# A decoder layer in three float32r passes: where its split weights and activations lie modulo 512 bytes

## The chip, the core and the metric

The kernel runs on one core of one Trainium2 chip. The metric is the device time of one execution in microseconds. Before the change it is 1091.87 us, the median of 3 runs (1091.37 to 1092.54). The profile is of one further execution.

## The reference, cut to what matters

One decoder layer on 256 tokens of width 2048: an input projection, eight heads of dilated window attention and eight heads of latent attention, an output projection, and an MLP with a squared ReLU, each between two RMSNorms. All inputs are float32.

```python
h = _rmsnorm(x, norm_attn_pre)
a_q, a_k, a_v, c_q, c_kv, k_r = split(h @ w_in)        # 2048 -> 3*1024 + 512 + 512 + 64
a_out = dilated window attention of (a_q, a_k, a_v)    # 8 heads x 128
q_b = _rmsnorm(c_q) @ w_uq; kv = _rmsnorm(c_kv) @ w_ukv
b_out = causal attention of (q_b, kv, k_r)             # 8 heads x 128
x = x + _rmsnorm(concat(a_out, b_out) @ w_out, norm_attn_post)   # 2048 -> 2048
h = _rmsnorm(x, norm_mlp_pre)
u = square(relu(h @ w_up))                             # 2048 -> 8192
x = x + _rmsnorm(u @ w_down, norm_mlp_post)            # 8192 -> 2048
```

## The kernel before

**Three passes.** A float32 product is carried by three float32r passes. Each operand is split exactly into a part of 12 significant bits, called hi, and the rest, called lo; hi*hi, lo*hi and hi*lo are added up in PSUM. ScalarE (ACT) writes hi by a copy that rounds (L234), VectorE (DVE) writes lo as source minus hi (L235). For three tiles of the first chunk of `w_up` GpSimd (POOL) writes lo instead (`POOL_U`).

**Which operand is which.** The activations are the stationary operand: 128 tokens by 128 of the inner dimension, loaded into TensorE (PE) by a weight load, which the profile calls LDWEIGHTS and lists under the engine PEld. There is one such load for every matmul. The weights of the model are the moving operand: 512 columns of a split tile stream past (288 for the latent projection, 384 for `w_uq`). So while a matmul streams 2048 bytes of a split weight tile from each partition, the weight load of the next matmul reads 512 bytes of an activation from the same partition.

**Weight tiles.** There are 377 weight tiles, numbered in the order of use, of 1024 columns by 128 partitions in float32 (4096 bytes a partition) or less. `Weights.emit` loads tile i into one of 5 raw buffers with a DMA on SP's queue, then issues its split into one of 8 hi and 8 lo buffers (`W_BUFS`). `Weights.get(i)` is called when tile i is used, and emits up to tile i + 6 (`W_AHEAD`; 4 around the norms of the residual, `AHEAD_NORM`), but never more than `limit` = 8 tiles past the first one that isn't finished.

**Order.** The order on each engine is written out by hand. `proj` emits the matmuls of a chunk tile by tile, first for the token block 0 and then for block 1, and `Flow` puts the short steps of attention heads and norms between them. In the last chunk of `w_out` the last 5 tiles, and in the first of `w_up` the first 7, are used by block 0 as a whole before block 1 uses them (`APART`), so that `residual(0)` and `residual(1)` can run on DVE, ACT and POOL beside the matmuls. The MLP's down projection keeps its whole output in 8 PSUM banks (`y`); in its last group of 8 tiles (`g` = 15, tiles 369 to 376) each bank is finished by itself, and ACT squares it and DVE scales it while PE works on the next.

**Where tiles lie.** Tiles of a pool lie one behind the other in each partition: pools on the left side grow from low addresses, pools on the right from the top. In the program that is built from this kernel the addresses are, modulo 512 bytes:

| tile | role | residue |
|---|---|---|
| hi and lo of every weight tile | moving | 352 |
| `xT` hi and lo (q, k, v, latents) | stationary | 384 |
| `cqT` hi and lo (`w_uq`) | stationary | 384 |
| `mixT` hi and lo (`w_ukv`, `w_out`) | stationary | 480 |
| `hT` hi and lo (`w_up`) | stationary | 352 |
| `u` hi and lo (`w_down`) | stationary | 352 |

Steps inside a tile are multiples of 512 bytes, except in the latent projection, whose second half starts 1152 bytes on. So the distance from the moving to the stationary operand, modulo 512, is 32 for q, k, v, c_q and `w_uq`; 32 and 416 in turn for the latent c_kv; 128 for `w_ukv` and `w_out`; and 0 for the whole MLP.

Of the kernel before, what the change touches and what calls it, by code (L numbers as in the profile page):

```python
"""One decoder layer: dilated sliding-window heads and latent-attention heads side by side,
then a squared-ReLU MLP, each between two RMSNorms.

Float32 products are carried by three float32r passes: an operand is split exactly into
hi (12 significant bits) and lo (the rest), and hi*hi + hi*lo + lo*hi are accumulated.
Activations are the stationary operand (128 tokens), weights move 512 columns at a time.

The three dilated configurations share their scores, so their merged output is one softmax
in which a key counts once for each configuration that sees it: exp(s) * n = exp(s + ln n).
"""  # L10
# [44 lines left out]
def shape_constants():  # L55
    """Rotary frequencies and attention biases: they depend on the shapes alone."""
    fa = (THETA ** (-np.arange(0, RA, 2, dtype=np.float64) / RA)).astype(np.float32)
    fb = (THETA ** (-np.arange(0, RB, 2, dtype=np.float64) / RB)).astype(np.float32)
    freq = np.concatenate([-fa, fa, -fb, fb, fa, fa, fb, fb])
    i = np.arange(P)[:, None] + P  # L60
    j = np.arange(2 * P)[None, :]
    dist = i - j
    count = np.zeros((P, 2 * P))
    for window, dil in CONFIGS:
        count += (dist >= 0) & (dist <= window) & (dist % dil == 0)
    bias_a = np.where(count > 0, np.log(np.maximum(count, 1)) / SCALE_A, NEG)
    bias_b = np.where(dist >= 0, 0.0, NEG)
    out = np.concatenate([np.broadcast_to(freq, (P, 192)), bias_a, bias_b], axis=1)
    return np.ascontiguousarray(out.astype(np.float32))


# Weight tiles: raw ones that loads fill ahead, split ones, and how far ahead of their use they are
# split. AHEAD_NORM: the same while the norms around the residual need the vector engine; POOL_U:
# tiles of that stretch whose lo part gpsimd computes.
RAW_BUFS, W_BUFS, W_AHEAD, AHEAD_NORM = 5, 8, 6, 4
POOL_U = (3, 5, 7)
# Tiles in which block 0 goes before block 1: the last of w_out, the first of w_up.
APART = (5, 7)
# The first tiles are split by k-tile, and their lo parts are used last.
FINE = 6  # L80
FIRST_KPTS = [1, 1] + [2] * 7
# x^T by pieces: k-tiles, and the weight tiles loaded by then.
X_PIECES = ((1, 1), (1, 2), (2, 3), (3, 4), (3, 6), (3, 7), (3, 7))
# Products of zeros that raise the tensor engine's clock while the first loads are on their way.
# [3 lines left out]
# Pauses between the steps of a chain, by the flow's clock. DA, DB: a head's, after the transposes,  # L88
# the scores, the maximum, the exponentials, the normalisation, the probabilities' transpose.
# [11 lines left out]
class Flow:  # L101
    """Order of emission: projections fill the tensor engine, and chains of short dependent
    steps (an attention head, a norm) put their steps between them, each a while after the last."""
# [26 lines left out]
    def until(self, reached):  # L130
        """Emit steps of chains until this holds."""
        while not reached():
            c = min(self.chains, key=lambda c: c[0])
            self.clock = max(self.clock, c[0])
            self._step(c)

    def finish(self, *chains):
        """Emit until these chains have ended."""
        self.until(lambda: not any(c in self.chains for c in chains))


class Weights:
    """Weight tiles in the order of their use: loaded and split some tiles ahead."""
# [11 lines left out]
    def emit(self, upto):  # L155
        upto = min(upto, self.done.index(False) + self.limit, len(self.specs))
        while len(self.tiles) < upto:
            i = len(self.tiles)
            src, nk, n = self.specs[i]
            raw = self.pool.tile([P, CW], F32, tag="raw", bufs=RAW_BUFS, name=f"raw{i}")  # L160
            hi = self.pool.tile([P, CW], F32R, tag="hi", bufs=self.bufs, name=f"hi{i}")
            lo = self.pool.tile([P, CW], F32R, tag="lo", bufs=self.bufs, name=f"lo{i}")
            w = nk * n

            def v(t):
                return t[:, :w].rearrange("p (k n) -> p k n", k=nk)

            self.nc.sync.dma_start(out=v(raw), in_=src.rearrange("(k p) n -> p k n", p=P))
            cuts = [(k * n, (k + 1) * n) for k in range(nk)] if i < FINE else [(0, w)]
            for o, e in cuts:  # L170
                self.split_fn(hi[:, o:e], lo[:, o:e], raw[:, o:e], i in self.on_pool)
            self.tiles.append((v(hi), v(lo)))
# [9 lines left out]
class Chunk:  # L182
    """512 or so columns of a weight: its tiles as (index, first k-tile, k-tiles)."""
# [9 lines left out]
    def plan(self, n):  # L193
        """Put the next n tiles into the order of use."""
        for kp in self.kpts[len(self.tiles):len(self.tiles) + n]:
            k = sum(self.kpts[:len(self.tiles)])
            src = self.src[k * P:(k + kp) * P, self.c0:self.c0 + self.n]
            self.tiles.append((self.weights.plan(src, kp, self.n), k, kp))


def layer(nc, tc, io):
# [5 lines left out]
    con = pool("con", "left")  # L207
    xp = pool("xp", "left")
# [64 lines left out]
    def in_order(n, apart=(0, 0)):  # L273
        """(tile, block) pairs; block 0 goes before block 1 in the first and the last `apart` tiles."""
        f, l = apart[0], n - apart[1]
        return ([(t, b) for b in range(NB) for t in range(f)] + [(t, b) for t in range(f, l) for b in range(NB)]
                + [(t, b) for b in range(NB) for t in range(l, n)])

    def proj(aT, chs, name, order=None, need=None):
        """tokens x chunks into PSUM; yields (chunk, block, banks) as each ends."""  # L280
# [31 lines left out]
    def rstd_of(ss, n, width, name):  # L312
        """(sum / width + eps) ** -0.5, [128, n]."""
# [10 lines left out]
    xT = [pa.tile([P, KD, S], F32R, name=f"xT_{w}") for w in ("hi", "lo")]  # L324
    gcol = con.tile([P, 8], F32, name="gcol")
# [13 lines left out]
    def x_piece(k0, nk):  # L339
        """k-tiles of x^T, each with its gain as the last column."""  # L340
# [40 lines left out]
    def tables():  # L381
        """Rotary tables: sin (its first half negated) and cos, [128, block, 96] each."""
# [22 lines left out]
    def rope(tmp_pool, dst, src, half, nh, first, name):  # L405
        """dst, src [128, block, nh, 2 * half]; tables from column `first`."""
# [12 lines left out]
    def softmax_pv(wk, dl, sc, bias, scale, v, head, name):  # L419
        """sc [128, 384]: scores of block 0 on keys 0..127, then of block 1 on keys 0..255."""  # L420
# [83 lines left out]
    def latent(c, i, n, pl):  # L504
        """Transposed latent with its gain, split; its norm's factor goes on after the product."""
# [27 lines left out]
    # shared rotary key, in the upper or the lower 64 rows, zero elsewhere  # L533
# [14 lines left out]
    latT["q"] = [pb.tile([P, 4, S], F32R, name=f"cqT_{w}") for w in ("hi", "lo")]  # L548
    q_chain = flow.start(latent(cq, 1, "q", pb), 2.0)
# [84 lines left out]
    def residual(b):  # L634
        """x += y * rstd * gain; x * gain of the next norm, transposed and split."""
# [42 lines left out]
    for ns in ((0, 1), (2,), (3,)):  # L678
# [4 lines left out]
        for c, b, acc in proj(mixT, [ch_o[n] for n in ns], f"o{ns[0]}", order, heads_done):  # L683
            n = ns[c]
            if not late:
# [4 lines left out]
                late["hT"] = [hp.tile([P, KD, S], F32R, name=f"hT_{w}") for w in ("hi", "lo")]  # L690
# [22 lines left out]
    def split_u(g):  # L713
        if g == 0:
            uh, ul = [wp.tile([P, CW], F32R, tag=w, bufs=W_BUFS, name=f"u{w}0").rearrange("p (k s) -> p k s", k=4)
                      for w in ("hi", "lo")]
        else:
            uh, ul = [dpl["dp"].tile([P, 4, S], F32R, tag=f"u{w}", bufs=2, name=f"u{w}{g}") for w in ("hi", "lo")]
        split(uh.rearrange("p k s -> p (k s)"), ul.rearrange("p k s -> p (k s)"), uT[g].rearrange("p k s -> p (k s)"))
        return uh, ul  # L720
# [27 lines left out]
    def down_mm(u, g, kk, b, ns):  # L748
        """One k-tile into these 512 columns, ns in one tile of the weight."""
# [9 lines left out]
    def spare(i, n):  # L759
        """512 columns in two uT tiles that have been used."""  # L760
# [9 lines left out]
    def final(b):  # L770
        """The last columns' square closes the sum; x += y * gain * rstd."""
# [66 lines left out]
def arrays_of(inputs):  # L838
    """The inputs as the kernel reads them: x also transposed, with its gain; other gains by column."""
# [29 lines left out]
```

## Time and profile before

| what | value |
|---|---|
| median of 3 runs | 1091.87 us |
| the profiled execution, first to last instruction (span) | 1089.3 us |
| PE busy | 1074.7 us, 4978 matmuls |
| PEld busy | 890.1 us, 4978 weight loads |
| DVE busy | 568.0 us |
| ACT busy | 526.9 us |
| POOL busy | 14.2 us |
| DMA | 203.09 MB, mean 186 GB/s |
| mean granted TensorE clock | 0.996 |

Times are in microseconds from the start of the span. A matmul's duration in a row contains its way through the array, which overlaps the next matmul; what a stream of matmuls costs is the distance between their starts, called the pitch below. Busy PE is the union of such durations and says nothing of the pitch. A row with "x2" or "x4" merges that many instructions. "PEclk" is the clock that TensorE was granted, as a share of full speed.

### The profile page before, as it was taken

What the parts mean: (1) busy time and instruction counts of PE and PEld (TensorE: products, weight loads), DVE (VectorE), ACT (ScalarE), POOL (GpSimd) and SP (SyncE); (2) the same over time, 40 slices, a digit from 0 to 9 for tenths busy, and PEclk for the clock granted to TensorE, in tenths of its full rate; (3) what the DMA queues carried; (4) which work ended last, traced back from release to release, by engine and by line L of the source; (5) the groups of instructions that cost most, each with busy time, mean ns of one, the idle gap of its engine ahead of it and who ended that gap; (6) DMA issues with size and microseconds to landing.
All of it is one profiled execution on the core that took longest, in us unless ns stands there. A gap on an engine that the chain in (4) does not pass through costs nothing.

```text
span 1089.3 us, 13045 instructions
## 1 busy us (share of the span) xinstructions
PE 1074.7 (99%) x4978; PEld 890.1 (82%) x4978; DVE 568.0 (52%) x706; ACT 526.9 (48%) x700; POOL 14.2 (1%) x20
## 2 busy tenths in 40 slices
PE   9999999999999899999999999999999999999996
PEld 6888889888888688888888888888888888888885
DVE  6576446477554864444444444445544454445444
ACT  6655446565453464554445544454444444444442
POOL 0000000000000300000000000000000000000000
PEclk9999999999999999999999999999999999999998
DMA  9874546455376376566665666646655567655532
GB/s 318 304 251 146 145 125 214 149 167 166 100 257 205 97 232 181 168 191 196 191 181 169 189 198 191 185 165 208 195 193 193 192 193 232 194 194 194 193 119 78
DMA packets 89967, 203.09 MB, mean 186 GB/s; under 512 B 6832, under 2 KB 11440, under 8 KB 89648
## 3 DMA queue, kind: packets, MB, share of 16 engines
q1 hardware_dynamic: 89472, 201.89, 58.7%
q8 instruction: 39, 0.64, 0.3%
q10 hardware_dynamic: 432, 0.37, 0.1%
q14 instruction: 24, 0.20, 0.0%
HBM read 200.13 MB, written 2.10 MB: 186 GB/s over the span
## 4 chain that ended last, share of the span: by engine, by line
PE 97%; issue 1%; DVE 1%; DMA 1%; ACT 0%; POOL 0%; DVEq 0%; POOLq 0%; ACTq 0%
PE y L226 31%; PE acc_u L226 31%; PE acc_o L226 8%; PE acc_v L226 4%; PE acc_k L226 4%; PE acc_q L226 4%; PE acc_ckv L226 2%; PE acc_cq L226 2%; PE acc_ukv L226 2%; PE acc_uq L226 2%; PE rt L230 1%; PE sc_b L226 1%; PE sc_a L226 0%; PE o_a L226 0%; PE o_b L226 0%
## 5 line engine op out<-in xcount | busy, mean ns | idle before, releaser
L235 DVE TENSOR_TENSOR lo<-raw,hi 128x1024 fp32r<-128x1024 f32 (+3 forms) x378 | 447.4, 1190 | 445.9 <-ACT hi L234 444.8
L234 ACT ACTIVATE hi<-raw 128x1024 fp32r<-128x1024 f32 (+3 forms) x381 | 387.9, 1026 | 344.3 <-PE y L226 180.1
L226 PE MATMUL acc_u<-hi,hT_hi 128*128 128x512 f32 x512 | 203.3, 397 | 0.0
L226 PE MATMUL acc_u<-hi,hT_lo 128*128 128x512 f32 x512 | 200.1, 391 | 0.0
L226 PE MATMUL acc_u<-lo,hT_hi 128*128 128x512 f32 x512 | 199.8, 390 | 0.0
L226 PE MATMUL y<-hi,uhi 128*128 128x512 f32 x512 | 199.4, 389 | 0.0
L226 PE MATMUL y<-lo,uhi 128*128 128x512 f32 x512 | 199.2, 389 | 0.0
L226 PE MATMUL y<-hi,ulo 128*128 128x512 f32 x512 | 160.3, 389 | 0.0
L226 PEld LDWEIGHTS acc_u<-hi,hT_lo 128*128 128x128 f32 x512 | 96.4, 188 | 20.6
L226 PEld LDWEIGHTS y<-hi,ulo 128*128 128x128 f32 x512 | 96.1, 188 | 20.1
L226 PEld LDWEIGHTS y<-hi,uhi 128*128 128x128 f32 x512 | 96.1, 188 | 19.9
L226 PEld LDWEIGHTS y<-lo,uhi 128*128 128x128 f32 x512 | 96.1, 188 | 19.9
L226 PEld LDWEIGHTS acc_u<-lo,hT_hi 128*128 128x128 f32 x512 | 96.6, 189 | 19.0
L226 PEld LDWEIGHTS acc_u<-hi,hT_hi 128*128 128x128 f32 x512 | 96.5, 188 | 18.9
L226 PE MATMUL acc_o<-hi,mixT_hi 128*128 128x512 f32 x128 | 52.3, 409 | 0.0
L226 PE MATMUL acc_o<-hi,mixT_lo 128*128 128x512 f32 x128 | 50.6, 396 | 0.0
L226 PE MATMUL acc_o<-lo,mixT_hi 128*128 128x512 f32 x128 | 50.5, 394 | 0.0
L736 ACT ACTIVATE r<-acc_u,rstd_pre 128x512 f32<-128x512 f32 x32 | 21.9, 689 | 53.5 <-PE acc_u L226 53.5
L226 PEld LDWEIGHTS acc_o<-hi,mixT_lo 128*128 128x128 f32 x128 | 24.1, 188 | 6.0 <-DVE mixT_lo L235 0.4
L226 PEld LDWEIGHTS acc_o<-hi,mixT_hi 128*128 128x128 f32 x128 | 24.1, 189 | 5.1 <-ACT mixT_hi L234 0.2
L226 PEld LDWEIGHTS acc_o<-lo,mixT_hi 128*128 128x128 f32 x128 | 24.2, 189 | 4.9
L711 ACT ACTIVATE uT<-rt 128x512 f32<-128x512 f32 x32 | 19.1, 597 | 17.2 <-PE rt L230 17.1
(192 smaller groups left out, 1019.2 us busy)
## 6 DMA issues: line engine op xcount, KB each, us to landing
raw<-in_w_up SPq DMA_DIRECT2D x128, 512.0 KB, 4.2
raw<-in_w_down SPq DMA_DIRECT2D x128, 512.0 KB, 4.5
raw<-in_w_in SPq DMA_DIRECT2D x55, 512.0 KB, 5.0
raw<-in_w_out SPq DMA_DIRECT2D x32, 512.0 KB, 4.3
raw<-in_w_in SPq DMA_DIRECT2D x16, 288.0 KB, 2.8
raw<-in_w_ukv SPq DMA_DIRECT2D x8, 512.0 KB, 4.3
raw<-in_w_uq SPq DMA_DIRECT2D x8, 384.0 KB, 3.3
x<-in_x SPq DMA_DIRECT2D x8, 256.0 KB, 6.2
```

The costliest lines, as they stand in the source:

```text
L226: nc.tensor.matmul(out, a, b, start=start, stop=stop)
L230: nc.tensor.transpose(out, a, ident)
L234: nc.scalar.activation(hi, src, AF.Copy)
L235: (nc.gpsimd if pool else nc.vector).tensor_tensor(out=lo, in0=src, in1=hi.bitcast(F32), op=OP.subtract)
L711: nc.scalar.activation(uT[j][:, :, b * P:(b + 1) * P], t.rearrange("p (k s) -> p k s", k=4), AF.Square)
L736: nc.scalar.activation(r, acc[0], AF.Relu, scale=rstd2[b])
```

## The change

Three things are changed; the rest of the diff takes out comments and docstrings (some as blank lines), so that line numbers move by up to 9.

```diff
-RAW_BUFS, W_BUFS, W_AHEAD, AHEAD_NORM = 5, 8, 6, 4
+RAW_BUFS, W_BUFS, W_AHEAD, AHEAD_NORM = 5, 7, 6, 4
+SHIFT, H_LO, U_HI, U_LO = 16, 8, 4, 12
...
-            hi = self.pool.tile([P, CW], F32R, tag="hi", bufs=self.bufs, name=f"hi{i}")
-            lo = self.pool.tile([P, CW], F32R, tag="lo", bufs=self.bufs, name=f"lo{i}")
+            s = i % 8 * SHIFT
+            hi = self.pool.tile([P, CW + 8 * SHIFT], F32R, tag="hi", bufs=self.bufs, name=f"hi{i}")[:, s:s + CW]
+            lo = self.pool.tile([P, CW + 8 * SHIFT], F32R, tag="lo", bufs=self.bufs, name=f"lo{i}")[:, s:s + CW]
...
     con = pool("con", "left")
+    con.tile([P, 32], F32, name="con_pad")
...
+    pa.tile([P, 104], F32, name="pa_pad")
...
+    pb.tile([P, 104], F32, name="pb_pad")
...
-                late["hT"] = [hp.tile([P, KD, S], F32R, name=f"hT_{w}") for w in ("hi", "lo")]
+                late["hT"] = [hp.tile([P, KD * S + s], F32R, name=f"hT_{w}")[:, s:].rearrange("p (k s) -> p k s", k=KD)
+                              for w, s in (("hi", 0), ("lo", H_LO))]
...
         if g == 0:
-            uh, ul = [wp.tile([P, CW], F32R, tag=w, bufs=W_BUFS, name=f"u{w}0").rearrange("p (k s) -> p k s", k=4)
-                      for w in ("hi", "lo")]
+            uh, ul = [wp.tile([P, CW + 8 * SHIFT], F32R, tag=w, bufs=W_BUFS, name=f"u{w}0")[:, s:s + CW]
+                      for w, s in (("hi", U_HI), ("lo", U_LO))]
         else:
-            uh, ul = [dpl["dp"].tile([P, 4, S], F32R, tag=f"u{w}", bufs=2, name=f"u{w}{g}") for w in ("hi", "lo")]
+            uh, ul = [dpl["dp"].tile([P, CW + 128], F32R, tag=f"u{w}", bufs=2, name=f"u{w}{g}")[:, s:s + CW]
+                      for w, s in (("hi", U_HI), ("lo", U_LO))]
```

**The residues.** A buffer for a split tile is 512 bytes longer, and tile i starts (i mod 8) times 64 bytes into it. With the pads the weights lie at 480, 32, 96, 160, 224, 288, 352 and 416 in turn, `xT`, `cqT`, `mixT` and the hi part of `hT` at 480, the lo part of `hT` at 0, `u` hi at 496 and `u` lo at 16. The distance from moving to stationary operand then takes, about equally often, the 8 multiples of 64 in the projections up to `w_out`; the multiples of 64 (two matmuls in three) and 32 more (one in three) in `w_up`; and 16 and 48 more than a multiple of 64 in `w_down`.

**The buffers.** 7 hi and 7 lo buffers in place of 8, and with them `limit` = 7.

**The order.** PE and SP execute the same instructions in the same order as before. On the other engines the smaller `limit` moves these: the split of tile 123 (the third of `w_up`) goes behind ACT's first square of the last `w_out` chunk, and on DVE into the chain of `residual(0)`, behind its first two updates; ACT's hi of tile 128 goes from among the squares of block 0 to behind the last hT part of block 1, and POOL's lo of tile 128 behind block 0's last rstd; around the last chunk of `w_up` and the second u split, a few splits and activations change places by one; and the split of the last tile, 376, goes from ahead of the squares and gains of banks y00, y01, y10 and y11 to behind them, on ACT and on DVE.

More of the change, by code (lines that the diff above doesn't have):

```diff
@@ L714, in split_u @@
         if g == 0:
-            uh, ul = [wp.tile([P, CW], F32R, tag=w, bufs=W_BUFS, name=f"u{w}0").rearrange("p (k s) -> p k s", k=4)
-                      for w in ("hi", "lo")]
-        else:
-            uh, ul = [dpl["dp"].tile([P, 4, S], F32R, tag=f"u{w}", bufs=2, name=f"u{w}{g}") for w in ("hi", "lo")]
-        split(uh.rearrange("p k s -> p (k s)"), ul.rearrange("p k s -> p (k s)"), uT[g].rearrange("p k s -> p (k s)"))
-        return uh, ul
+            uh, ul = [wp.tile([P, CW + 8 * SHIFT], F32R, tag=w, bufs=W_BUFS, name=f"u{w}0")[:, s:s + CW]
+                      for w, s in (("hi", U_HI), ("lo", U_LO))]
+        else:
+            uh, ul = [dpl["dp"].tile([P, CW + 128], F32R, tag=f"u{w}", bufs=2, name=f"u{w}{g}")[:, s:s + CW]
+                      for w, s in (("hi", U_HI), ("lo", U_LO))]
+        split(uh, ul, uT[g].rearrange("p k s -> p (k s)"))
+        return [t.rearrange("p (k s) -> p k s", k=4) for t in (uh, ul)]
     evac = []
```

## The prediction

> **What bounds the kernel now.** First the page: who is busy, and what the chain that ended last is made of. Then the pitch of the matmuls, read from the PE rows of the timeline in each stage.
>
> ```profile
> PE 1074.7 (99%) x4978; PEld 890.1 (82%) x4978; DVE 568.0 (52%) x706; ACT 526.9 (48%) x700; POOL 14.2 (1%) x20
> ...
> PE 97%; issue 1%; DVE 1%; DMA 1%; ACT 0%; POOL 0%; DVEq 0%; POOLq 0%; ACTq 0%
> ...
> L226 PE MATMUL acc_u<-hi,hT_hi 128*128 128x512 f32 x512 | 203.3, 397 | 0.0
> ...
> L226 PE MATMUL y<-hi,uhi 128*128 128x512 f32 x512 | 199.4, 389 | 0.0
> ...
> L226 PE MATMUL acc_o<-hi,mixT_hi 128*128 128x512 f32 x128 | 52.3, 409 | 0.0
> ```
>
> The chain is 97% PE, so the number of matmuls times their pitch is the time. By such counts there are 3 x 512 = 1536 matmuls of 512 columns into acc_u and as many into y, and 384 into acc_o; q, k and v have 192 each, c_q and `w_ukv` 96 each. The order on PE does not change, so only the pitch and PE's waits can. One stretch without interruption from each stage:
>
> ```profile
> 55.02 0.40 PE L226 MATMUL acc_v<-hi,xT_hi 128*128 128x512 f32 x1
> ...
> 57.82 0.40 PE L226 MATMUL acc_v<-hi,xT_hi 128*128 128x512 f32 x1
> ...
> 310.11 0.40 PE L226 MATMUL acc_o<-lo,mixT_hi 128*128 128x512 f32 x1
> ...
> 314.06 0.39 PE L226 MATMUL acc_o<-hi,mixT_hi 128*128 128x512 f32 x1
> ...
> 570.21 0.39 PE L226 MATMUL acc_u<-lo,hT_hi 128*128 128x512 f32 x1
> ...
> 571.57 0.39 PE L226 MATMUL acc_u<-lo,hT_hi 128*128 128x512 f32 x1
> ...
> 834.77 0.39 PE L226 MATMUL y<-hi,uhi 128*128 128x512 f32 x1
> ...
> 852.91 0.39 PE L226 MATMUL y<-hi,uhi 128*128 128x512 f32 x1
> ```
>
> 12 steps in 2.80 us are 233.3 ns each for acc_v; 17 steps in 3.95 us are 232.4 for acc_o; 6 in 1.36 us are 226.7 for acc_u; 80 in 18.14 us are 226.8 for y (the windows row below has the count: 81 with the one at its start). Same shape, same type, and still 6 ns apart. Is it the neighbours?
>
> ```profile
> 55.02:57.82 2.80, 2.80 (x13) 1.00 0.98 332
> 570.21:578.37 8.16, 8.16 (x41) 1.00 0.41 109
> 310.11:314.06 3.95, 3.95 (x18) 1.00 0.94 354
> 834.77:852.90 18.13, 18.13 (x81) 1.00 0.61 195
> ```
>
> The granted clock (the 1.00) is the same. The DMA share (second last) is 0.41 beside one pitch of 226.7 and 0.61 beside the other, so it isn't DMA traffic alone. What does go with the pitch is the layout: the distance between the two operands modulo 512 bytes is 32 for acc_v, 128 for acc_o and 0 for acc_u and y. And both are read at once, since each weight load starts with the matmul ahead of its own:
>
> ```profile
> 499.99 0.39 PE L226 MATMUL acc_u<-lo,hT_hi 128*128 128x512 f32 x1
> 499.99 0.19 PEld L226 LDWEIGHTS acc_u<-hi,hT_lo 128*128 128x128 f32 x1
> 500.21 0.39 PE L226 MATMUL acc_u<-hi,hT_lo 128*128 128x512 f32 x1
> 500.22 0.19 PEld L226 LDWEIGHTS acc_u<-hi,hT_hi 128*128 128x128 f32 x1
> ```
>
> One more row set tells what a matmul costs without any loss. At 375 us, behind a long gap, the clock is briefly halved:
>
> ```profile
> 375.24 0.63 PE L226 MATMUL acc_u<-lo,hT_hi 128*128 128x512 f32 x1
> 375.67 0.63 PE L226 MATMUL acc_u<-hi,hT_lo 128*128 128x512 f32 x1
> 376.10 0.63 PE L226 MATMUL acc_u<-hi,hT_hi 128*128 128x512 f32 x1
> 376.52 0.63 PE L226 MATMUL acc_u<-lo,hT_hi 128*128 128x512 f32 x1
> ```
>
> 3 steps in 1.28 us are 427 ns. Half of that, 213.5, is what the array alone would need at full clock; the MLP loses 13 ns a matmul to something else, q, k and v lose 20.
>
> **The change, part by part.** *Residues.* I read the three pitches as a cost of the distance: 0 is the cheap place (226.7), 32 and 128 are ordinary ones (233.3 and 232.4). The new layout gives up the single distance 0 of the whole MLP and visits all of them. For an ordinary distance I take the middle of the two measured, 232.8, so +6.1 ns. One distance in eight, those next to 0, I leave at the cheap pitch. MLP: 3072 x 7/8 x 6.1 ns = +16.4 us. In turn, an eighth of the other 512-column matmuls reaches distance 0: q, k, v and c_q (672) save 672/8 x 6.6 ns = 0.6 us, `w_out` and `w_ukv` (480) save 480/8 x 5.7 ns = 0.3 us; with the narrow ones about 1.0. Bounds for the unseen distances: upwards, all of the MLP at 233.3, with nothing saved elsewhere, is 3072 x 6.6 = +20.3 us. Downwards, no loss at all would be 213.5 everywhere: 3072 x 13.2 + 672 x 19.8 + 480 x 18.9 = 63 us less. I take the ordinary price because it is the one seen at two distances, both of which are in the new set, and the cheap one has been seen at one alone.
>
> The Trainium skill (SBUF — State Buffer, "Who interferes with whom") says that TensorE reads the moving operand and the weight load through two independent ports and never waits on anyone; by it the residues would move nothing and the first part of the sum would be 0. The Trainium skill (TensorE: Matmul & The Clock Gate, "Back-to-back issue gap") gives N/2.4 + 2.5 ns, an estimate of 215.8 ns for 512 columns. The trace agrees with neither: 226.7 and 233.3 are both above, and they differ between stages.
>
> *Seven buffers.* ACT already waits for PE to free the next buffer, and DVE waits for ACT:
>
> ```profile
> ACT hi L234 <- PE y L226: 180.1, 118, 1.7
> ...
> DVE lo L235 <- ACT hi L234: 444.8, 309, 5.4
> ```
>
> One buffer fewer makes each such split start one tile later, 12 x 226.7 = 2.7 us, out of a lead of six tiles or 16 us; behind it in ACT's queue stand evacuations of the chunk that PE is still computing, which wait for PE anyway. So this costs nothing, except where the lead isn't there. That is so in two places.
>
> At the end, tile 376 can only be split once the first tile of its group is free, and stands behind the square and gain of y11:
>
> ```profile
> 1070.31 0.60 ACT L765 ACTIVATE junkd<-y 128x512 bf16<-128x512 f32 x1 [2.03 <-PE y L226]
> 1070.81 0.19 ACT L765 ACTIVATION_READ_ACCUMULATOR junkd<-y 128x1 f32 x1
> ...
> 1059.37 1.06 ACT L234 ACTIVATE hi<-raw 128x1024 fp32r<-128x1024 f32 x1 [1.66 <-PE y L226]
> 1060.46 1.23 DVE L235 TENSOR_TENSOR lo<-raw,hi 128x1024 fp32r<-128x1024 f32 x1 [1.49 <-ACT hi L234]
> ...
> 1070.05 0.39 PE L226 MATMUL y<-hi,uhi 128*128 128x512 f32 x1
> ```
>
> ACT is free at 1071.0, hi is there at 1072.1 and lo at 1073.3. PE starts y02 at 1070.05 and needs the lo of its fourth tile after ten matmuls, at 1072.3: a stall of +1.0 us, now on the chain (bounds 0 and 2).
>
> At the residual, POOL and DVE collide. An update of x by DVE takes 1.42 us for two when POOL is idle, and 3.49 beside POOL's lo:
>
> ```profile
> 354.29 1.42 DVE L643 SCALAR_TENSOR_TENSOR x<-yg,rstd_post,x 128x512 f32<-128x512 f32 x2 [0.67 <-POOL rstd_post L317]
> ...
> 358.82 2.99 DVE L643 SCALAR_TENSOR_TENSOR x<-yg,rstd_post,x 128x512 f32<-128x512 f32 x1
> ...
> 369.63 2.35 POOL L235 TENSOR_TENSOR lo<-raw,hi 128x1024 fp32r<-128x1024 f32 x1
> 369.69 3.49 DVE L643 SCALAR_TENSOR_TENSOR x<-yg,rstd_post,x 128x512 f32<-128x512 f32 x2 [0.67 <-POOL rstd_post L317]
> ...
> 373.93 1.09 PE L230 MATMUL ht<-ident,yg 128*128 128x128 f32 x4 [3.93 <-DVE yg L646]
> ```
>
> That POOL op is tile 128. It moves to behind the last rstd of block 0, so block 1's update should be 2.1 us shorter, PE's gap of 3.93 us about half as long, and the halved clock behind it may go (about 5 matmuls at +200 ns, 1.0 us): up to -3.1 us. Against it, DVE's lo of tile 123 (1.23 us) now stands in block 0's chain, ahead of the update that ran at 356.8; pushed back, the steps up to hT_lo may land on POOL's first lo (the update beside it took 2.99 against 0.7), so up to +1.2 + 2.3 = +3.5. I take -1.0 for this place, nearer the gain, because only the gain lies on a gap that PE shows.
>
> *Sum.* 16.4 - 1.0 + 1.0 - 1.0 = +15.4 us on the span of 1089.3, which makes 1104.7. The median of the runs is 2.6 above that span; with it the forecast is 1107.3, say 1107. Its own range goes from 1097 (three eighths of the distances cheap: 3072 x 5/8 x 6.1 = 11.7, less 2.9 elsewhere and 3.1 at the residual) to 1116 (+20.3, +1 and +3.5).
>
> **The rivals.** *Faster: the spread removes the loss.* Distance 0 would then itself be a bad place where two equal residues meet, and most others better. For it: 13 ns are still lost at 0, and nothing in the trace says that this part is inherent. Against it: 32, 128 and the mix of 32 and 416 are the only other distances seen; the first two are dearer by 6 ns. If half of the loss goes, 63/2 = 31 us, the time is 1061; if all, 1029. It wins as soon as the mean pitch over all distances is under 226.7 in the MLP.
>
> *Slightly faster: nearly all new distances are like 0*, and 32 and 128 the exceptions. The MLP stays, 7/8 of 672 x 6.6 + 480 x 5.7 = 6.3 us are saved: 1085. Against it: two of two distances away from 0 would be exceptions.
>
> *The change doesn't do what it says.* The pitch differs by stage for another reason (the ranges of addresses, the PSUM banks), and residues are no lever; then only the buffers act, -1.0 + 1.0: 1092, within their bounds of about 3 either way. The Trainium skill's rule on the ports (SBUF — State Buffer, "Who interferes with whom") would have it so. Against it: acc_u and y use different banks and tiles, and share only the distance, and the pitch.
>
> **How the numbers follow.** The forecast, slower by an ordinary distance price, gets 0.66; the spread that removes the loss 0.18; nearly all like 0 gets 0.09; no lever 0.07, of which 0.04 within 0.2% (2.2 us, about what a measurement of this kernel can tell from no change), 0.01 faster and 0.02 slower. So faster 0.18 + 0.09 + 0.01 = 0.28, same 0.04, slower 0.68. The range must leave out no more than 2 in 10: from 1076, which takes in the cases at 1085 and 1092 and the mildest of the removal, to 1117. Left out are most of the removal and a little above.
>
> **What would show it.** In the changed profile the timeline of y and acc_u: within one tile all distances are fixed, so the pitch must change from tile to tile, with a period of 8 tiles, mean 231 to 233; tiles with index 0 modulo 8 in acc_v (distance 0) at 227, the others near 233. At the end a PE wait of about 1 us for DVE's lo ahead of the y02 bank's last tile. At the residual POOL's third lo behind rstd_pre, DVE's two updates for block 1 near 1.4 us, PE's gap under 3 us. Wrong would be: MLP pitches under 226.7 in most tiles (the first rival), a pitch without a period of 8 tiles (no lever), or waits of PE for lo tiles in mid-stage, which would mean that the seven buffers run dry.

## The result, and the profile after

The changed kernel takes 1103.55 us (median of 4 runs, 1102.72 to 1104.6) against 1092.2 us for the kernel before beside it (median of 4, 1091.37 to 1092.54). The ratio is 1.0108, with a 95% interval from 1.0094 to 1.0121: it is slower by 11.35 us. The profiled execution has a span of 1101.9 us, 12.6 more than before.

First the page of the kernel after, with the lines that answer to those shown of before: engines, chain, and the costliest groups (busy us, mean ns of one, idle time ahead).

```profile
PE 1086.5 (99%) x4978; PEld 888.6 (81%) x4978; DVE 565.8 (51%) x706; ACT 532.2 (48%) x700; POOL 15.8 (1%) x20
...
PE 95%; DMA 1%; DVE 1%; issue 1%; ACT 1%; POOL 0%; DVEq 0%; POOLq 0%; SPq 0%; ACTq 0%
...
L231 PE MATMUL acc_u<-hi,hT_hi 128*128 128x512 f32 x512 | 204.6, 400 | 0.0
L231 PE MATMUL y<-lo,uhi 128*128 128x512 f32 x512 | 202.1, 395 | 0.7 <-DVE lo L240 0.7
```

PE is busy for 11.8 us more with the same number of matmuls, and the only wait in these groups is 0.7 us. So the pitch has to be looked at. The best rows for that are windows cut from the start of one matmul to the start of another (0.03 us ahead of both), the same matmuls in every kernel: then the lengths can be compared. Columns: length, PE busy (matmuls, one of them running in from before), granted clock, DMA share, GB/s. Before, for acc_u and for y:

```profile
415.40:723.60 308.20, 308.20 (x1413) 1.00 0.62 184
...
739.07:1059.14 320.07, 320.07 (x1413) 1.00 0.60 194
```

And the kernel after, the same 1412 matmuls each (in acc_u 1300 of 512 columns and 28 groups of 4 transposes):

```profile
413.97:727.45 313.48, 313.48 (x1413) 1.00 0.62 181
...
743.20:1070.11 326.91, 326.91 (x1413) 1.00 0.57 191
```

There is no idle time in any of the four, and the clock is 1.00 in all. acc_u is longer by 5.28 us and y by 6.84, that is 4.1 and 4.8 ns a matmul. Over all 1536 of each it makes 6.2 + 7.4, about 13.7 us.

Does the pitch go with the tile, as it must if the distance sets it? Five tiles of acc_v of the kernel after, 12 matmuls each. The distance falls by 64 from row to row: 256, 192, 128, 64, 0.

```profile
60.68:63.42 2.74, 2.74 (x13) 1.00 0.60 182
63.42:66.19 2.77, 2.77 (x13) 1.00 0.70 199
66.19:68.98 2.79, 2.79 (x13) 1.00 0.74 203
68.98:71.78 2.80, 2.80 (x13) 1.00 0.89 299
71.78:74.52 2.74, 2.74 (x13) 1.00 1.02 366
```

The pitch is 228.3 ns at 256 and at 0, 230.8 at 192, and 232.5 to 233.3 at 128 and 64. The DMA share is highest (1.02) beside a cheap tile. It does change with the tile; but 256 is as cheap as 0.

The waits that the buffers were to move, in the timelines of the kernel after (start, us, idle time in brackets). The end, on PE, DVE and ACT:

```profile
1083.38 0.39 PE L231 MATMUL y<-hi,uhi 128*128 128x512 f32 x1
1084.50 0.51 PE L231 MATMUL y<-lo,uhi 128*128 128x512 f32 x1 [0.73 <-DVE lo L240]
...
1083.21 1.23 DVE L240 TENSOR_TENSOR lo<-raw,hi 128x1024 fp32r<-128x1024 f32 x1 [0.25 <-ACT hi L239]
...
1082.13 1.05 ACT L239 ACTIVATE hi<-raw 128x1024 fp32r<-128x1024 f32 x1
```

From start to start it is 1.12 us where 0.23 are usual: +0.89 us. The split of the last tile now stands behind the squares, and PE waits for its lo part.

The residual: block 1's update on DVE and the gap ahead of its transposes on PE.

```profile
370.39 1.41 DVE L650 SCALAR_TENSOR_TENSOR x<-yg,rstd_post,x 128x512 f32<-128x512 f32 x2 [0.67 <-POOL rstd_post L322]
...
370.86 0.40 PE L231 MATMUL acc_u<-hi,hT_lo 128*128 128x512 f32 x1
372.56 0.63 PE L235 MATMUL ht<-ident,yg 128*128 128x128 f32 x4 [1.29 <-DVE yg L653]
...
373.26 0.39 PE L231 MATMUL acc_u<-lo,hT_hi 128*128 128x512 f32 x1
373.49 0.40 PE L231 MATMUL acc_u<-hi,hT_lo 128*128 128x512 f32 x1
```

The two updates take 1.41 us where they took 3.49 beside POOL's lo, the gap is 1.29 us where it was 3.93, and behind it the matmuls start 0.23 us apart: the halved clock is gone.

### The profile page after: what moved, and what is told of

It reads as the page before. It is cut to its first block, busy times and chain, and to the rows that moved or that the text cites. A ratio compares the mean times of both kernels' runs of the same rounds, so it can differ in the third digit from the quotient of the medians.

```text
span 1101.9 us, 13043 instructions
## 1 busy us (share of the span) xinstructions
PE 1086.5 (99%) x4978; PEld 888.6 (81%) x4978; DVE 565.8 (51%) x706; ACT 532.2 (48%) x700; POOL 15.8 (1%) x20
## 4 chain that ended last, share of the span: by engine, by line
PE 95%; DMA 1%; DVE 1%; issue 1%; ACT 1%; POOL 0%; DVEq 0%; POOLq 0%; SPq 0%; ACTq 0%
PE y L231 32%; PE acc_u L231 30%; PE acc_o L231 8%; PE acc_k L231 4%; PE acc_v L231 4%; PE acc_q L231 4%; PE acc_ckv L231 2%; PE acc_cq L231 2%; PE acc_ukv L231 2%; PE acc_uq L231 2%; PE rt L235 1%; PE sc_b L231 1%; DMA raw<-in_w_in 1%; ACT hi L239 1%; DVE lo L240 1%
## 5 line engine op out<-in xcount | busy, mean ns | idle before, releaser
L231 PE MATMUL y<-lo,uhi 128*128 128x512 f32 x512 | 202.1, 395 | 0.7 <-DVE lo L240 0.7
L231 PE MATMUL y<-hi,ulo 128*128 128x512 f32 x512 | 162.9, 394 | 0.0
L745 ACT ACTIVATE r<-acc_u,rstd_pre 128x512 f32<-128x512 f32 x32 | 21.9, 688 | 15.4 <-PE acc_u L231 15.4
L231 PE MATMUL acc_q<-hi,xT_hi 128*128 128x512 f32 x64 | 26.7, 418 | 1.6 <-ACT hi L239 1.6
```

Source lines behind the costliest of these rows:

```text
L231: nc.tensor.matmul(out, a, b, start=start, stop=stop)
L745: nc.scalar.activation(r, acc[0], AF.Relu, scale=rstd2[b])
```

## The experiments

Three theories are told apart. D: the distance from the moving to the stationary operand sets the pitch. B: the time goes with the number of buffers, seven in place of eight. C: what costs is that the distance changes from tile to tile; constant distances would all be alike.

**The buffers alone.** The kernel before with seven buffers:

```diff
-RAW_BUFS, W_BUFS, W_AHEAD, AHEAD_NORM = 5, 8, 6, 4
+RAW_BUFS, W_BUFS, W_AHEAD, AHEAD_NORM = 5, 7, 6, 4
```

> The kernel before with 7 split buffers in place of 8, layout as before. If the distance modulo 512 sets the price (theory D): MLP pitch stays at 226.7 ns; at the residual PE's gap of 4.32 us between two starts shrinks to about 1.7 as in the changed kernel, at the end one gap of 1.1 us appears; together -3.3 + 0.9 = -2.4, so about 1089.8 us. If the seven buffers are what costs (theory B): most of the 11.35 us are here, about 1103 us.

Measured: 1091.0 us (11 runs), ratio 0.9989 [0.998, 0.9998]. Its y stretch and its way from the first acc_u matmul to the 200th:

```profile
739.02:1059.09 320.07, 320.07 (x1413) 1.00 0.60 196
...
361.95:415.35 53.40, 50.00 (x233) 1.00 0.60 189
```

The pitch is that of before, to the last digit (320.07 us). The second row holds the residual: before it is 55.88 us, so the shorter gap saves 2.5 us. In this profile nearly all of it is given back in stalls, of which the prediction had only the one at the end; by the medians 1.3 us are left. Beside that one there is a stall in acc_o and one ahead of the second up-chunk's transposes:

```profile
309.16 0.50 PE L226 MATMUL acc_o<-hi,mixT_lo 128*128 128x512 f32 x1 [0.59 <-DVE mixT_lo L235]
...
392.85 0.33 PE L230 MATMUL rt<-ident,r 128*128 128x128 f32 x1 [0.79 <-ACT r L736]
```

B falls: the buffers are worth -1 us in all, and not +11.

**The distance at 0 everywhere, nothing in turn.** The three pads alone, with 8 buffers:

```diff
     con = pool("con", "left")
+    con.tile([P, 32], F32, name="con_pad")
...
+    pa.tile([P, 104], F32, name="pa_pad")
...
+    pb.tile([P, 104], F32, name="pb_pad")
```

> The kernel before with the three pads alone, 8 buffers, no shifts: the distance is 0 in every stage of 512 columns. Theory D: acc_q, acc_k, acc_v and acc_cq fall from 233.3 to 226.7 ns, acc_o and acc_ukv from 232.4 to 226.7; 672 x 6.6 + 480 x 5.7 = 7.2 us less, about 1085 us. If instead it is the change of distance from tile to tile that costs, and a constant one is as good as another (theory C): no pitch moves, 1092 us.

Measured: 1087.01 us (5 runs), ratio 0.9952 [0.9939, 0.9966]. 95 steps of acc_v, at distance 32 in the kernel before and at distance 0 here. Before:

```profile
51.49:73.66 22.17, 22.17 (x96) 1.00 0.84 272
```

With the pads:

```profile
51.15:72.69 21.54, 21.54 (x96) 1.00 0.74 240
```

The pitch falls from 233.4 to 226.7 ns, the MLP's. C has nothing for this, since the distance is constant in both. That the pitch follows the stage and not the layout falls too. Of the 7.2 us that were expected 5.3 came: added up start by start in the two traces, without the steps beside waits and other matmuls, acc_v saves 6.7 ns a matmul, but acc_o only 4.3.

**The MLP at 128, and at 256.** In the kernel before, `hT` and `u` are moved by 128 bytes, with the weights where they were; only the group of `u` that lies in the weights' own buffers stays. The second kernel moves them by 256 (64 floats).

```diff
+                hp.tile([P, 32], F32, name="hp_pad")
...
-            uh, ul = [dpl["dp"].tile([P, 4, S], F32R, tag=f"u{w}", bufs=2, name=f"u{w}{g}") for w in ("hi", "lo")]
+            uh, ul = [dpl["dp"].tile([P, CW + 128], F32R, tag=f"u{w}", bufs=2, name=f"u{w}{g}")[:, 32:32 + CW] for w in ("hi", "lo")]
+            uh, ul = [t.rearrange("p (k s) -> p k s", k=4) for t in (uh, ul)]
```

> The kernel before with hT moved by 128 bytes and u by 128 bytes (all groups but the first): the distance in the MLP is 128, constant, for 2940 matmuls. Theory D: their pitch goes from 226.7 to about 232.4 ns, +16.8 us, about 1109 us. Theory C: the distance is constant, so the pitch stays at 226.7: 1092 us.

> As the one at 128, but hT and u moved by 256 bytes. The changed kernel's acc_v rows have 227 ns at distances 0 and 256 alike: if the period is 256, the pitch stays at 226.7 and the time at 1092 us; if only 0 modulo 512 is cheap (what the prediction assumed), +17 us, about 1109 us.

Measured: 1109.58 us (4 runs), ratio 1.0157 [1.0143, 1.0171], at 128; 1092.12 us (10 runs), ratio 1.0 [0.9991, 1.0009], at 256. The y stretch at 128:

```profile
748.99:1076.75 327.76, 327.76 (x1413) 1.00 0.58 189
```

And at 256:

```profile
739.87:1059.95 320.08, 320.08 (x1413) 1.00 0.59 194
```

One constant distance costs 17 us in the whole kernel, and another nothing. So C falls, and 256 is as good as 0: the distance modulo 512 was the wrong measure.

**The map, in steps of 32 and of 4.** The changed kernel with steps of 32 bytes from tile to tile and no shift of `h` and `u`; then with steps of 4 bytes, `h` and `u` shifted by 16. In both the weights' buffers are 256 bytes longer than before, in place of 512.

```diff
-SHIFT, H_LO, U_HI, U_LO = 16, 8, 4, 12
+SHIFT, H_LO, U_HI, U_LO = 8, 0, 0, 0
```

> The changed kernel with steps of 32 bytes in place of 64, and hi and lo parts of h and u alike at the same residue, so that every weight tile has one distance for all its matmuls and each stage visits the multiples of 32. If the price is a function of the distance modulo 256 (theory D), the pitch by tile is the same in acc_v, acc_o, acc_u and y: 226.7 ns at 0, about 233 at 32, 64 and 128; and no tile is under 226. If the changed kernel's MLP is dear because two distances follow each other within a tile, acc_u and y fall below their 231.5 of the changed kernel on average. Time about 1100 us.

> The same with steps of 4 bytes: distances from 28 bytes below 0 to 16 above it, modulo 256. If the cheap place is a range of a 64-byte line or more, all tiles stay near 226.7 ns and the time is about 1085 us; if it is the exact address, only distance 0 is at 226.7 and the rest near 233, about 1108 us.

Measured: 1106.11 us and 1107.57 us, one run each, beside 1092.85 us before. The weights start at 480 and steps of 32 or 4 bytes on. From the first kernel three of eight successive tiles of acc_v, 12 matmuls each, at the distances -64, 128 and 0 (modulo 256):

```profile
54.57:57.33 2.76, 2.76 (x13) 1.00 0.90 285
...
60.14:62.94 2.80, 2.80 (x13) 1.00 0.52 137
...
71.32:74.05 2.73, 2.73 (x13) 1.00 1.03 382
```

By twelfths that is 230, 233.3 and, at 0, 227.5 ns; the five tiles left out, at the other multiples of 32, are at 232.5 to 234.2. The cheap tile again has the largest DMA share beside it (1.03). In y of the same run the tiles at 0 and 128 take 227.5 and 233.3 as well, in acc_u 228.3 and 232.5: at starts on multiples of 32 bytes the distance sets the price, in each of these stages alike. The stationary operand starts at 480 throughout this run, so a step of the distance is also a step of the weights' own start; the two are told apart only at 0, 32, 128 and 256, which occur with other starts too.

The second kernel, in steps of 4, tells them apart further. In acc_v, with the stationary operand at 480 again, the distances -4, -28 and 0:

```profile
52.06:54.91 2.85, 2.85 (x13) 1.00 0.60 161
...
68.89:71.63 2.74, 2.74 (x13) 1.00 1.00 339
71.63:74.37 2.74, 2.74 (x13) 1.00 1.04 383
```

Four bytes away from 0 the tile takes 237.5 ns, 28 bytes away 228.3, the same as at 0. In acc_u and y of this run the stationary operand starts at 496. Three tiles of acc_u, with the moving operand at 480, 496 and 500, that is at the distances 16, 0 and -4:

```profile
502.85:505.58 2.73, 2.73 (x13) 1.00 0.69 190
...
514.84:517.63 2.79, 2.79 (x13) 1.00 0.66 178
517.63:520.49 2.86, 2.86 (x13) 1.00 0.69 185
```

And a tile of y, with the moving operand at 480, distance 16:

```profile
802.60:805.40 2.80, 2.80 (x13) 1.00 0.53 184
```

They take 227.5, 232.5, 238.3 and 233.3 ns. So here distance 0, with both operands at 496, is not cheap: it costs 6 ns more than with both at 480. And the same two starts, 480 and 496, are cheap in acc_u and dear in y. What the steps of 4 follow better is the moving operand's own start: 4 bytes past a multiple of 16 (484, 500) a tile takes 235 to 238.3 ns in acc_v, acc_u and y, 12 bytes past (492, 508) 228.3 to 230, at six different distances. D as it stands holds for starts on multiples of 32 bytes; between them a rule isn't found here. No distance in the two maps has a mean under 226.7.

**Which of the two reads loses the rest.** At distance 0 a matmul still takes 226.7 ns. Two kernels with the pads alone, each with one operand of `w_down` read from one address only. In the first the moving operand is one column repeated 512 times (the other columns of `w_down` are left out), in the second the stationary operand is one column of `u` repeated 128 times (the other tokens are left out).

```diff
-                    mm(y[b][n], tok(u[x], kk, b), w[:, 0, o:o + 512],
+                    mm(y[b][n], tok(u[x], kk, b), w[:, 0, o:o + 1].to_broadcast([P, 512]),
```

```diff
-                    mm(y[b][n], tok(u[x], kk, b), w[:, 0, o:o + 512],
+                    mm(y[b][n], u[x][:, kk, b * P:b * P + 1].to_broadcast([P, P]), w[:, 0, o:o + 512],
```

> The kernel with the pads alone, but in w_down the moving operand is one column of the weight tile repeated 512 times (step 0); the other columns of w_down are left out, so the output differs. At distance 0 a matmul still takes 13 ns longer than the array needs. If that comes from the moving stream's reads (its own or where they meet the weight load's), the pitch of y falls to about 215 ns, 1536 x 11.5 = 17.7 us less; if it belongs to the swap of the stationary operand, it stays at 226.7.

> The kernel with the pads alone, but in w_down the stationary operand is one column of u repeated 128 times (step 0); the other tokens of u are left out, so the output differs. If the 13 ns left at distance 0 come from the two reads meeting, the pitch of y falls to about 215 ns, 17.7 us less; if they come from the moving stream alone, it stays at 226.7.

Measured: 1069.79 us and 1095.08 us, one run each. The y stretch with the moving operand fixed:

```profile
734.10:1038.85 304.75, 304.75 (x1413) 1.00 0.63 204
```

And with the stationary operand fixed:

```profile
735.53:1062.64 327.11, 327.11 (x1413) 1.00 0.59 190
```

304.75 us are 215.8 ns a matmul, 11 less than at distance 0, with the same weight loads beside it. So the rest of the loss is not the change of the stationary operand. The second kernel was to be at 215 if the two reads meet, and at 226.7 if the loss is the moving stream's own; it is at 231.7, a dear distance's pitch, and neither was right. A weight load that reads one address over and over goes with a higher pitch than one that runs along with the stream at distance 0; why is open. Whether the moving stream would lose the 11 ns without any weight load beside it wasn't tried and stays open.

**Turning between two cheap places.** The changed kernel with the weights at two residues 256 bytes apart in turn, and `h` and `u` unshifted:

```diff
-SHIFT, H_LO, U_HI, U_LO = 16, 8, 4, 12
+SHIFT, H_LO, U_HI, U_LO = 64, 0, 0, 0
...
-            s = i % 8 * SHIFT
+            s = i % 2 * SHIFT
```

> The changed kernel with the weights at two residues in turn, 256 bytes apart, and the parts of h and u all at one residue: the distance still changes from tile to tile, between 0 and 256. Theory D with period 256: the pitch is 226.7 ns in every stage, the time that of the pads alone with 7 buffers, 1087.0 - 1.3 = about 1086 us. If turning itself breaks a lock that a constant layout has (theory C): pitch near 231.5 as in the changed kernel, about 1103 us.

Measured: 1086.95 us (4 runs), ratio 0.9951 [0.9937, 0.9964]. Its acc_v and y stretches:

```profile
51.92:73.45 21.53, 21.53 (x96) 1.00 0.78 249
...
734.01:1054.09 320.08, 320.08 (x1413) 1.00 0.60 196
```

The residue changes with every tile, there are seven buffers, each 512 bytes longer as in the changed kernel, and the pitch is 226.7 ns in both stages. So neither the turning nor the buffers cost the changed kernel its time; what is left is where the operands start.

**The better version.** The pads alone with 8 buffers, and `limit` = 7 only while the norms of the residual run. It was to take the gain at the residual without the stalls elsewhere.

```diff
     # in residual, where block 1 restores the lead
             weights.ahead = W_AHEAD
+            weights.limit = W_BUFS
...
     # at the last chunk of w_out
                 weights.ahead = AHEAD_NORM
+                weights.limit = W_BUFS - 1
```

> The kernel with the pads alone and 8 buffers, but with the limit of split tiles ahead at 7 during the two residual chains alone, which puts GpSimd's third lo behind the rstd of block 0. From the kernels with 7 buffers: PE's gap before the transposes of block 1 falls from 4.29 us to about 1.7 between starts, the halved clock behind it goes (1 us); the gaps that 7 buffers brought elsewhere (in acc_o, before rt, at the last y02 tile) stay away. 1087.0 - 2.6 - 1.0 = about 1083.5 us. If moving GpSimd's op isn't what shortened the gap, 1087 us.

Measured: 1084.16 us (5 runs), ratio 0.9926 [0.9913, 0.994]. The gap at the residual:

```profile
365.24 1.42 DVE L646 SCALAR_TENSOR_TENSOR x<-yg,rstd_post,x 128x512 f32<-128x512 f32 x2 [0.67 <-POOL rstd_post L318]
...
367.40 0.99 PE L231 MATMUL ht<-ident,yg 128*128 128x128 f32 x4 [1.87 <-DVE yg L649]
```

DVE's updates are free of POOL here too, and the gap is 1.87 us. The stalls in acc_o and at the end are not there. But two things came otherwise than expected, in the profiled execution: behind the gap the clock is halved all the same, and PE's stall ahead of the second up-chunk's transposes is there.

```profile
368.00:370.80 2.80, 2.80 (x9) 0.50 0.00 1
...
387.30 0.66 PE L231 MATMUL rt<-ident,r 128*128 128x128 f32 x4 [0.61 <-ACT r L741]
```

The kernel is faster by 8 us than the one before, whose median beside it was 1092.29, and its slowest run (1085.42, the profiled one) is faster than the fastest with the pads alone (1086.5, beside a median of 1092.33 for the one before).

## Why the prediction was right, and where its sizes were off

It said 1107, slower because the MLP leaves the cheap place for places that mostly cost more. It is 1103.55, by that mechanism. What each place costs was in good part not as assumed.

- **Bound and lever: right.** PE's pitch carries the difference, and where the operands start sets it. Moving the stationary operand alone by 128 bytes made the kernel before slower by 17 us, and pads alone made it faster by 5. The rival that residues are no lever falls, and with it, for this kernel, the rule of the Trainium skill (SBUF — State Buffer, "Who interferes with whom") that the two reads are independent and TensorE waits on nobody: at the same clock 1412 matmuls of y take 320.07 or 327.76 us by the place of `u` alone. The rival that the spread removes the loss falls by the maps, where no distance has a mean under 226.7, and by the changed kernel's own MLP.
- **The price of the MLP: 16.4 us forecast, about 13.7 measured.** The term that was off is "One distance in eight, those next to 0, I leave at the cheap pitch", with the ordinary price for the other seven: 7/8 x 6.1 = 5.3 ns a matmul, where 4.1 and 4.8 were measured. No tile of y is at the cheap pitch. Two tiles of y, index 0 and 2 modulo 8, in the kernel after:

```profile
800.63:803.39 2.76, 2.76 (x13) 1.00 0.55 188
...
806.17:808.97 2.80, 2.80 (x13) 1.00 0.54 192
```

  That is 230 and 233.3 ns; the tiles 1 and 3 lie at 231.7, and with the fifth it begins again, a period of 4 tiles and not of 8. The ordinary price, 232.8, holds where acc_v reaches 64 and 128 (232.5 to 233.3). But the price repeats after 256 bytes, not 512; a distance of 192 costs less (230.8 in acc_v); and in the MLP each tile mixes two distances, in `w_down` with starts of `u` off the multiples of 32, for which nothing had been measured. That these errors have opposite signs kept the sum near.
- **The other stages: -1.0 forecast, about -1.6 measured.** With the period of 256 twice as many tiles hit a cheap place. In acc_v the 95 steps of before take 22.17 us, and in the changed kernel:

```profile
52.33:74.29 21.96, 21.96 (x96) 1.00 0.77 249
```

  That is 2.2 ns less a matmul. Added up start by start in the two traces, q, k, v and c_q together save 1.2 us, acc_o and `w_ukv` 0.4.
- **The end: +1.0 forecast, +0.89 measured,** with the split behind y11's square, as said.
- **The residual: -1.0 forecast, about -3.5 measured,** past its bound of -3.1. From the first acc_u matmul to the 200th, before:

```profile
359.52:415.40 55.88, 51.00 (x233) 0.97 0.56 179
```

  And after:

```profile
360.24:413.97 53.73, 50.80 (x233) 1.00 0.58 188
```

  It is 2.15 us shorter, though 200 matmuls in it cost 0.8 more by their pitch and the new stall at its end 0.6. The granted clock, 0.97 before and 1.00 after, shows the halved clock gone. The loss that was set against the gain, lo of tile 123 in block 0's chain, did come, but cost PE little. In the kernel after:

```profile
357.54 1.22 DVE L240 TENSOR_TENSOR lo<-raw,hi 128x1024 fp32r<-128x1024 f32 x1
...
364.34 0.66 PE L235 MATMUL ht<-ident,yg 128*128 128x128 f32 x4 [1.19 <-DVE hT_lo L240]
```

  PE's gap there is 1.19 us where before it was:

```profile
363.19 0.66 PE L230 MATMUL ht<-ident,yg 128*128 128x128 f32 x4 [0.95 <-DVE hT_lo L235]
```

  So the choice of -1.0, between the ends, was the mistake: the gain was on PE's path in full, and the 1.2 us on DVE mostly were not. The Trainium skill (SBUF — State Buffer, "Who interferes with whom") says that a DVE instruction with two SBUF inputs contends with a GpSimd instruction that reads SBUF; the trace agrees, 3.49 us beside POOL's lo and 1.41 without.
- **"So this costs nothing, except where the lead isn't there. That is so in two places": there were two more.** In the kernel after:

```profile
306.03 1.23 DVE L240 TENSOR_TENSOR lo<-raw,hi 128x1024 fp32r<-128x1024 f32 x1 [1.59 <-ACT hi L239]
...
307.64 0.50 PE L231 MATMUL acc_o<-hi,mixT_lo 128*128 128x512 f32 x1 [0.60 <-DVE mixT_lo L240]
...
391.05 0.66 PE L235 MATMUL rt<-ident,r 128*128 128x128 f32 x4 [0.45 <-ACT r L745]
```

  From start to start they lose some 0.75 and 0.6 us. Both show in the kernel with seven buffers alone as well. In the first, DVE waits 1.59 us for a split whose buffer came free later, and mixT_lo, which PE needs at once, stands behind that split. In the second, r stands on ACT behind two splits that wait 1.28 and 0.27 us for their loads. The prediction had counted only evacuations that wait for PE anyway.

The measured parts are 13.7 - 1.6 + 0.9 - 3.5 + 1.4 = +10.9 us, beside 11.35 between the medians. That the forecast of +15.4 came this near is partly luck: the MLP, the other stages and the residual were all forecast too dear, by 2.7, 0.6 and 2.5 us, and the two stalls that were left out put 1.4 back. The profiled executions lie 12.6 apart; of that, 1.2 us are at the start, where PE waits for ACT's first splits: in the first 51 us it was busy for 49.45 us before and for 48.25 after. The kernel with the pads alone and 8 buffers has it too in its profile (48.44), so this isn't put down to the change.

## What to carry over

Where a stream of matmuls has no idle time, read its pitch by tile and set it beside the starts of the two operands. In this kernel, with both on multiples of 32 bytes, distances of 0 and 256 took 226.7 to 228.3 ns and the others 230 to 234, and three pads of up to 416 bytes gained 5 us. Spreading addresses is no cure when one place is the best and can be kept: of the other places none was seen cheaper. And a smaller number of buffers is judged by each queue it reorders, for it can take a collision away in one place and put an urgent evacuation behind a split in another.

## What had not been expected of the hardware

- With both operands on multiples of 32 bytes the pitch goes with their distance, and 256 is as cheap as 0 (320.08 and 320.07 us for the same 1412 matmuls of y; 128: 327.76). Off these multiples distance isn't enough: with both operands at 496 a tile of acc_u takes 232.5 ns, and 4 bytes of the moving operand's start are worth 9 ns in acc_v (228.3 at 480, 237.5 at 484).
- A moving operand read from a single column runs at 215.8 ns for 512 columns. The Trainium skill (TensorE: Matmul & The Clock Gate, "Back-to-back issue gap") gives N/2.4 + 2.5 ns, for an isolated matmul, an estimate of 215.8: the trace agrees with it in this one stream, and in no stage with a real moving operand, where 226.7 was the least.
- A weight load that reads one column 128 times makes the matmuls beside it dearer (231.7 ns) than one that reads 128 columns at distance 0 (226.7).
